# A Strassen-Winograd output projection that opens with two direct products, with its activation operands formed a stage earlier

## The chip, the cores and the metric

The kernel runs on one core of a Trainium2 chip. The metric is the device time of one execution in microseconds (us). The core's engines are TensorE (PE; its weight loads are listed as PEld), VectorE (DVE), ScalarE (ACT), GpSimd (POOL) and SyncE (SP). Each takes its instructions in its own order and waits for the others at semaphores. DMAs are issued here from SP (weights), from POOL (accumulating loads) and from ACT (a few row broadcasts).

## The reference

One layer over x of 512 tokens by 2048 channels, all in float32. Two mixers A and B work on the normalised input; their gated sum goes through w_out, whose result the change is about:

```python
y_a = o_a @ w_br_a[i]
...
u = jax.nn.silu(layernorm(u, ln_g[i], ln_b[i])) * jax.nn.silu(z_b)
y_b = u @ w_br_b[i]
gate_a, gate_b = jnp.split(jax.nn.sigmoid(gate_logits + b_gate[i]), N_BRANCHES, axis=-1)
mixed = (gate_a * y_a + gate_b * y_b) @ w_out[i]
x = x + rmsnorm(mixed, g_post[i])
e = p[i] @ w_ple_proj[i]
x = x + rmsnorm(jax.nn.sigmoid(x @ w_ple_gate[i]) * e, g_ple[i])
```

## The kernel before, in words

Every matrix product is done in three matmuls. An operand is split into a high part (hi: a cast on ScalarE) and a low part (lo: operand minus hi, a subtraction on VectorE), and hi by hi, hi by lo and lo by hi are added in PSUM. Weights come by DMA and are split just ahead of their matmuls.

The program runs the stages one after the other: normalisation and transposes, heads of branch A, the convolution of branch B, the gate and output tiles of branch A, then branch B, w_out, and the last gemm with its norms. In branch B the normalised input hT (in hpool, 32 buffers) gives sixteen gate tiles (gate_b), and the convolved uT gives sixteen output tiles (yb, from w_br_b); each is 48 matmuls. When a yb tile is done, VectorE multiplies it by its gate (L818) and adds it to the tile of mixed (L820). In the order of the code, two gate tiles run ahead, then one gate tile and one yb tile in turn.

w_out multiplies mixed (512 by 2048) by a 2048 by 2048 matrix in Strassen-Winograd form: two column halves (jp) of seven products each, P1, Q5, P6, P7, P3, P2, Q4, instead of eight. The halves of the tokens and of the channels make four blocks of activations, and four of weights for each jp (B11, B12, B22, B21). The activation operands are A11 for P1, S1 for Q5, S2 for P6, S3 for P7, S4 for P3 (sums of blocks), A12 for P2 and A22 for Q4 (both in CC). split_a forms A11 and S1 between the last yb tiles and the start of w_out; split_b (S3, S2, S4) is stepped along with the pieces of P1 and Q5, split_c (CC) with those of P6, P7 and P3.

A *piece* is one quarter q of the rows of one product's weights: 128 by 1024, 512 KB, with 12 matmuls (L1034, L1035, L1036). Its source is either a loaded block (L950, from SP), or a sum. The sum t = B11 + B12 (VectorE, L964) serves Q5; then an accumulating DMA from POOL (L956) adds B22 to it for P6, and later B21 for Q4. t3 = B12 + B22 (L973) serves P7. split_piece makes a piece's hi (L1010) and lo (L1011); next_piece_sw keeps three or four pieces split ahead. Where a source is a sum, next_piece_sw issues its loads and at once, behind them, the sum.

Loads go to ring buffers (raw, three; shared with the stages before) or to rw (four); t has four buffers, the split halves lie in ring (w, four), wx (two) and later raw. A buffer is loaded anew when its last reader is done, and SP takes its loads in order. When products end, their PSUM tiles are copied (snap, L1056) or added on VectorE (L1060, L1064), squared and summed on ScalarE (L1079), and multiplied by the row g_post (grow, loaded from ACT's queue; L1080). After the last products come the norm and the transposes of the result (L1107, L1113).

The order of each engine's instructions is set at compile time by a scheduler that starts from the order of the code and moves instructions by their dependencies; what is written in a generator and stepped is spread over the steps by hand.

Of the kernel before, what the change touches and what calls it, by code (L numbers as in the profile page):

```python
# [15 lines left out]
P = 128  # L16
# [65 lines left out]
def _body(ctx, tc, A, out):  # L82
# [756 lines left out]
    def split_a():  # L839
        for k2 in range(4):  # L840
            ah = hpool.tile([P, T], F32R, tag="h", name="ah")
            al = hpool.tile([P, T], F32R, tag="h", name="al")
            s1 = slots.tile([P, T], F32, tag="s", name="sf")
            for n in range(2):
                kk = 2 * k2 + n
                while not (kk in added and kk + 8 in added):
                    yield
                c = slice(n * 256, n * 256 + 256)
                nc.vector.tensor_tensor(s1[:, c], mixed[kk][:, HI], mixed[kk + 8][:, HI], ALU.subtract)
                nc.scalar.copy(ah[:, c], mixed[kk][:, LO])  # L850
                nc.vector.tensor_tensor(al[:, c], mixed[kk][:, LO], ah[:, c].bitcast(F32), ALU.subtract)
                yield
            Sf[k2] = s1
            AW["A11"][k2] = (ah, al)
            AW["S1"][k2] = sw_split(hpool, "h", s1)
            yield

    def split_b():
        for k2 in range(4):
            s1 = Sf.pop(k2)  # L860
            s3_ = s3.tile([P, T], F32, tag="s3", name="sf")
            for n in range(2):
                kk = 2 * k2 + n
                c = slice(n * 256, n * 256 + 256)
                nc.vector.tensor_tensor(s3_[:, c], mixed[kk][:, LO], mixed[kk][:, HI], ALU.subtract)
                nc.vector.tensor_tensor(s1[:, c], s1[:, c], mixed[kk][:, LO], ALU.subtract)
            AW["S3"][k2] = sw_split(hpool, "h", s3_)
            yield
            AW["S2"][k2] = sw_split(hpool, "h", s1)
            for n in range(2):  # L870
                kk = 2 * k2 + n
                c = slice(n * 256, n * 256 + 256)
                nc.vector.tensor_tensor(s1[:, c], mixed[kk + 8][:, LO], s1[:, c], ALU.add)
            AW["S4"][k2] = sw_split(slots, "s", s1)
            yield
# [20 lines left out]
    lnp_ctx = ExitStack()
# [42 lines left out]
    entries = deque()  # L939
    sources = deque()  # L940
# [3 lines left out]

    def load(jp, blk, q):
        if early[0]:
            raw = ring.tile([P, 1024], F32, tag="raw", name="raw", bufs=3)
        else:
            raw = s3.tile([P, 1024], F32, tag="rw", name="rw", bufs=4)
        nc.sync.dma_start(raw, WO[jp, blk, q])  # L950
# [7 lines left out]
    def e_a(jp, q):  # L958
        early[0] = jp == 0
        b11 = load(jp, B11, q)  # L960
        b12 = load(jp, B12, q)
        early[0] = False
        t = tb[q] = s3.tile([P, 1024], F32, tag="t", name="t", bufs=4)
        nc.vector.tensor_tensor(t, b11, b12, ALU.add)  # L964
# [23 lines left out]
    def e_t(jp, q):
        return [tb[q]]

    def e_c(jp, q):
        return e_p2(jp, q) + [tb[q]]

    def split_piece():
# [4 lines left out]
        for m in range(2):  # L999
            if n < 8:  # L1000
# [142 lines left out]
    drain(gen)  # L1143
    u2 = [add(unit(S3_, "u2"), ps["P6"][t], s1[t]) for t in range(2)]
# [5 lines left out]
    ps = run(("P2", "Q4"))  # L1150
# [186 lines left out]
```

## Time and profile before

| | |
|---|---|
| median of 3 runs | 2549.19 us (2548.08 to 2549.82) |
| profiled execution | 2548.13 us, span 2546.4 us |
| granted TensorE clock, mean | 0.998 |
| busy: PE / PEld / DVE / ACT / POOL | 98 / 80 / 65 / 42 / 6 % of the span |
| DMA moved | 279.45 MB, mean 110 GB/s |
| w_out begins | at 2188 us (last L818 at 2188.14, first matmul at 2188.98) |

Times in the profile are microseconds from the start of the span, unless marked ns. "Idle before, releaser" is the time for which an engine stood still just ahead of an instruction, and the instruction or DMA that let it go. Lines are those of the kernel before unless the change is spoken of.

### The profile page before, as it was taken

The page shows a single profiled execution, that of the slowest core. Times are in us where ns is not written, and L with a number is a line of the kernel's source. Part 1 is how long each engine was busy: PE and PEld are TensorE (multiplying, and loading weights), DVE is VectorE, ACT ScalarE, POOL GpSimd, SP SyncE. Part 2 cuts the span into 40 slices and gives each one's busy share as a digit, 9 for nine tenths or more (in the row PEclk, how much of TensorE's full clock was granted, in tenths as well). Part 3 has the DMA queues.
Part 4 walks back from the last instruction along what each step waited for, and adds up shares of the span by engine and source line. Part 5 has one row for each costly group of instructions (what it writes and reads, how often), then busy time and mean ns, then how long its engine had stood idle before and what let it go on. Part 6 is the DMA issues. An engine that isn't in the chain of part 4 may idle for free.

```text
span 2546.4 us, 32634 instructions
## 1 busy us (share of the span) xinstructions
PE 2503.4 (98%) x12202; PEld 2032.5 (80%) x12202; DVE 1650.9 (65%) x3092; ACT 1058.2 (42%) x2083; POOL 140.4 (6%) x151
## 2 busy tenths in 40 slices
PE   8999999999999999999999999999999999899998
PEld 7878787777878777888888888887888888687886
DVE  6766767666676765977786868947423333787744
ACT  6655455455545545322222222225422222454532
POOL 0100000000000000000000000002000000000000
PEclk9999999999999999999999999999999999999999
DMA  6322222222222222333333333342322223577642
GB/s 256 118 90 71 84 74 80 79 78 84 71 83 72 83 69 81 103 101 106 98 104 100 103 108 96 108 161 91 100 98 93 99 91 99 165 218 213 216 173 75
DMA packets 85406, 279.45 MB, mean 110 GB/s; under 512 B 9472, under 2 KB 9728, under 8 KB 85248
## 3 DMA queue, kind: packets, MB, share of 16 engines
q1 hardware_dynamic: 81792, 266.89, 31.3%
q0 software_dynamic: 2304, 8.39, 1.9%
q10 hardware_dynamic: 1152, 2.10, 0.3%
q8 instruction: 95, 1.56, 0.3%
q14 instruction: 63, 0.52, 0.1%
HBM read 262.66 MB, written 14.68 MB: 109 GB/s over the span
## 4 chain that ended last, share of the span: by engine, by line
PE 84%; DVE 9%; ACT 2%; issue 2%; DMA 2%; POOL 0%; SPq 0%; DVEq 0%; POOLq 0%; ACTq 0%
PE g L180 22%; PE g L178 22%; PE g L176 22%; DVE prod L589 2%; DVE w L124 2%; PE f L1191 2%; PE f L1192 2%; PE f L1190 2%; DVE VT L590 2%; PE psS L467 1%; PE f L1035 1%; PE f L1036 1%; PE f L1034 1%; DVE cv L404 1%; PE psB L462 1%
## 5 line engine op out<-in xcount | busy, mean ns | idle before, releaser
L180 PE MATMUL g<-hh,w 128*128 128x512 f32 x2320 | 919.4, 396 | 13.2 <-DVE w L124 13.2
L178 PE MATMUL g<-hl,w 128*128 128x512 f32 x2320 | 915.9, 395 | 0.0
L176 PE MATMUL g<-hh,w 128*128 128x512 f32 x2320 | 914.5, 394 | 0.0
L124 DVE TENSOR_TENSOR w<-raw,w 128x512 fp32r<-128x512 f32 x780 | 547.8, 705 | 491.8 <-ACT w L123 490.7
L123 ACT CAST w<-raw 128x512 fp32r<-128x512 f32 x780 | 479.1, 620 | 899.2 <-PE g L180 822.6
L180 PEld LDWEIGHTS g<-hh,w 128*128 128x128 f32 x2320 | 436.7, 188 | 107.0 <-DVE w L124 21.4
L178 PEld LDWEIGHTS g<-hl,w 128*128 128x128 f32 x2320 | 436.6, 188 | 87.3 <-issue 1.6
L176 PEld LDWEIGHTS g<-hh,w 128*128 128x128 f32 x2320 | 436.6, 188 | 83.7 <-issue 0.2
L671 DVE SCALAR_TENSOR_TENSOR uc<-sg,vec,uc 128x483 f32<-128x483 f32 (+15 forms) x480 | 351.3, 734 | 14.2 <-ACT uc L668 4.3
L404 DVE SCALAR_TENSOR_TENSOR cv<-g,vec,cv 128x511 f32<-128x511 f32 x144 | 107.0, 743 | 32.9 <-ACT cv L402 32.3
L180 PE MATMUL g<-uh,w 128*128 128x512 f32 x256 | 100.9, 394 | 0.0
L176 PE MATMUL g<-oh,w 128*128 128x512 f32 x256 | 100.9, 394 | 0.0
L178 PE MATMUL g<-ol,w 128*128 128x512 f32 x256 | 100.9, 394 | 0.0
L180 PE MATMUL g<-oh,w 128*128 128x512 f32 x256 | 100.9, 394 | 0.0
L176 PE MATMUL g<-uh,w 128*128 128x512 f32 x256 | 100.9, 394 | 0.0
L178 PE MATMUL g<-ul,w 128*128 128x512 f32 x256 | 100.9, 394 | 0.0
L589 DVE TENSOR_TENSOR prod<-UT,VT 128x2 f32<-128x2 f32 (+30 forms) x248 | 87.8, 354 | 7.2
L1034 PE MATMUL f<-wsp,oph 128*128 128x512 f32 x192 | 74.9, 394 | 3.2 <-ACT wsp L1010 3.2
L1035 PE MATMUL f<-wsp,oph 128*128 128x512 f32 x192 | 75.7, 394 | 1.5 <-DVE wsp L1011 1.5
L1191 PE MATMUL f<-w,xh 128*128 128x512 f32 x192 | 75.1, 391 | 0.1
L1036 PE MATMUL f<-wsp,opl 128*128 128x512 f32 x192 | 75.1, 391 | 0.0
L1192 PE MATMUL f<-w,xl 128*128 128x512 f32 x192 | 75.0, 390 | 0.0
(297 smaller groups left out, 2678.2 us busy)
## 6 DMA issues: line engine op xcount, KB each, us to landing
raw<-in_w_in SPq DMA_DIRECT2D x290, 512.0 KB, 3.3
raw<-in_w_ple_gate SPq DMA_DIRECT2D x40, 512.0 KB, 4.0
rw<-in_w_out SPq DMA_DIRECT2D x36, 512.0 KB, 5.0
raw<-in_w_br_a SPq DMA_DIRECT2D x32, 512.0 KB, 3.3
raw<-in_w_br_b SPq DMA_DIRECT2D x32, 512.0 KB, 3.2
t<-in_w_out POOLq DMA_DIRECT2D x16, 512.0 KB, 7.3
x<-in_x SPq DMA_DIRECT2D x8, 512.0 KB, 9.4
pe_dram<-e_sb SPq DMA_DIRECT2D x16, 256.0 KB, 5.6
```

The lines of the kernel that those rows point to most:

```text
L123: nc.scalar.copy(hi, rq)
L124: nc.vector.tensor_tensor(lo, rq, hi.bitcast(F32), ALU.subtract)
L176: mm(ps, wh, rh, start=(k == 0), stop=False)
L178: mm(ps, wh, rl, start=False, stop=False)
L180: mm(ps, wl, rh, start=False, stop=(k == NK - 1))
L404: nc.vector.scalar_tensor_tensor(y[:, s:], ps[:, 0:T - s], vv(w0 + 3 - s), y[:, s:], ALU.mult, ALU.add)
L589: nc.vector.tensor_tensor(pv_, um, vm, ALU.mult)
L671: nc.vector.scalar_tensor_tensor(y[:, s:], u[:, 0:T - s], vv(w0 + TAPS - 1 - s), y[:, s:], ALU.mult, ALU.add)
L1035: mm(ps, lh, wl[:, c], start=False, stop=False)
L1036: mm(ps, ll, wh[:, c], start=False, stop=kk == 7)
L1191: mm(ps[tt], lh, wl, start=False, stop=False)
L1192: mm(ps[tt], ll, wh, start=False, stop=k == NK - 1)
```

## The change

Three things are changed.

1. In branch B eight gate tiles run ahead instead of two (six of the first eight, and all later ones, in the pool s2 instead of slots), so the last eight yb tiles stand one after the other, and hT's buffers are free before them. In these tiles combine(k2) forms A11, CC, S1, S2 and S4 for k2 = 0, 1, 2, one step every 12 matmuls. combine(3) and the splits of S3 stand beside P1 and P2, two steps for each piece.
2. The first column half begins with P1 and P2 in turn, straight from loaded B11 and B21. Then Q5 runs alone, with B11 loaded a second time beside B12 for t; then P6, P7, P3 as before; then Q4. P2's result is finished early. The first half has 24 plain loads instead of 20; the accumulating ones are as before, 16 in all. The second half keeps its order.
3. An entry is now two steps: its loads, and a function that does its sum. The loads of an entry are issued two entries ahead of its sum (started). Only the first three loads use the ring's raw buffers, and the pieces up to the ninth alternate between ring and wx. The rows of x for the last norm (xr) go to slots.

```diff
-    def evac_gate(dst, i, col):
+    def evac_gate(dst, i, col, pool=None):
         def f(ps):
-            gt = slots.tile([P, T], F32, tag="s", name="gt")
+            gt = (pool or slots).tile([P, T], F32, tag="s2" if pool else "s", name="gt")
...
-    def split_a():
...
+    def combine(k2):
+        ah = hpool.tile([P, T], F32R, tag="h", name="ah")
+        al = hpool.tile([P, T], F32R, tag="h", name="al")
+        for kk, c in halves(k2):
+            while not (kk in added and kk + 8 in added):
+                yield
+            nc.scalar.copy(ah[:, c], mixed[kk][:, LO])
+            nc.vector.tensor_tensor(al[:, c], mixed[kk][:, LO], ah[:, c].bitcast(F32), ALU.subtract)
+            yield
+        AW["A11"][k2] = (ah, al)
+        for kk, c in halves(k2):
+            CC[kk] = sw_split(hpool, "h", mixed[kk + 8])
+            yield
+        s1 = slots.tile([P, T], F32, tag="s", name="sf")
+        for kk, c in halves(k2):
+            nc.vector.tensor_tensor(s1[:, c], mixed[kk][:, HI], mixed[kk + 8][:, HI], ALU.subtract)
+        AW["S1"][k2] = sw_split(hpool, "h", s1)
+        yield
+        s3_ = slots.tile([P, T], F32, tag="s", name="sf")
+        s4 = slots.tile([P, T], F32, tag="s", name="sf")
+        for kk, c in halves(k2):
+            nc.vector.tensor_tensor(s3_[:, c], mixed[kk][:, LO], mixed[kk][:, HI], ALU.subtract)
+            nc.vector.tensor_tensor(s1[:, c], s1[:, c], mixed[kk][:, LO], ALU.subtract)
+        yield
+        for kk, c in halves(k2):
+            nc.vector.tensor_tensor(s4[:, c], mixed[kk + 8][:, LO], s1[:, c], ALU.add)
+        AW["S2"][k2] = sw_split(slots, "s", s1)
+        yield
+        AW["S4"][k2] = sw_split(slots, "s", s4)
+        Sf[k2] = s3_
+        yield
+
+    def split_mixed():
+        for k2 in range(3):
+            yield from combine(k2)
+
+    def split_s3():
         for k2 in range(4):
-            ah = hpool.tile([P, T], F32R, tag="h", name="ah")
-            al = hpool.tile([P, T], F32R, tag="h", name="al")
...
-            AW["S1"][k2] = sw_split(hpool, "h", s1)
...
-    def split_b():
-        for k2 in range(4):
...
-    def split_c():
-        for kk in range(8):
-            CC[kk] = sw_split(*((slots, "s") if kk < 4 else (s3, "s3")), mixed[kk + 8])
+            AW["S3"][k2] = sw_split(s3, "s3", Sf.pop(k2))
             yield
 
...
-    gate_b_tile(order[0])
-    gate_b_tile(order[1])
+    AHEAD = 8
+
+    def gate_b_tile(i, pool):
+        gemm_cm(w_in_tile(GATE_TILE0 + 16 + i), hT, evac_gate(gate_b, i, 16 + i, pool))
+
+    gate_b_tile(order[0], None)
+    gate_b_tile(order[1], None)
     jobs.append(finish)
+    for n in range(2, AHEAD):
+        gate_b_tile(order[n], s2)
     for n, i in enumerate(order):
-        if n + 2 < NK:
-            gate_b_tile(order[n + 2])
-        elif n == NK - 2:
-            jobs.append(lambda: spawn(split_a(), 6, "mix"))
         gemm_cm(A["w_br_b"][i], uT, evac_yb(i))
+        if n + AHEAD < NK:
+            gate_b_tile(order[n + AHEAD], s2)
+        elif n + AHEAD == NK:
+            jobs.append(lambda: spawn(split_mixed(), 12, "mix"))
...
+    started = deque()
...
     def load(jp, blk, q):
-        if early[0]:
+        loads[0] += 1
+        if loads[0] <= 3:
             raw = ring.tile([P, 1024], F32, tag="raw", name="raw", bufs=3)
         else:
             raw = s3.tile([P, 1024], F32, tag="rw", name="rw", bufs=4)
         nc.sync.dma_start(raw, WO[jp, blk, q])
         return raw
...
+    def e_p1p2(jp, q):
+        two = [load(jp, B11, q), load(jp, B21, q)]
+        return lambda: two
+
+    def sum_t1(jp, q):
         b11 = load(jp, B11, q)
         b12 = load(jp, B12, q)
-        early[0] = False
-        t = tb[q] = s3.tile([P, 1024], F32, tag="t", name="t", bufs=4)
-        nc.vector.tensor_tensor(t, b11, b12, ALU.add)
-        return [b11, t]
+
+        def f():
+            t = tb[q] = s3.tile([P, 1024], F32, tag="t", name="t", bufs=4)
+            nc.vector.tensor_tensor(t, b11, b12, ALU.add)
+            return [b11, t]
+        return f
+
+    def e_q5(jp, q):
+        f = sum_t1(jp, q)
+        return lambda: f()[1:]
 
     def e_63(jp, q):
...
-            if n < 8:
+            if n < 9:
...
     def next_piece_sw():
         ahead = 3 if count[0] < 10 else 4
-        while len(pieces) < ahead and (sources or entries):
-            while len(sources) < 2 and entries:
-                sources.extend(entries.popleft()())
+        while len(pieces) < ahead and (sources or entries or started):
+            while len(sources) < 2 and (entries or started):
+                while entries and len(started) < 2:
+                    started.append(entries.popleft()())
+                sources.extend(started.popleft()())
             split_piece()
...
-                xr[tt, j] = unit(HP_, "xr")
+                xr[tt, j] = unit(SLOT, "xr")
...
-    for e, jp in ((e_a, 0), (e_b, 0), (e_c, 0), (e_a, 1), (e_63, 1), (e_p2, 1), (e_p7, 1), (e_t, 1)):
+    for e, jp in ((e_p1p2, 0), (e_q5, 0), (e_b, 0), (e_q4, 0), (sum_t1, 1), (e_63, 1), (e_p2, 1), (e_p7, 1), (e_t, 1)):
         stage(e, jp)
 
-    gen = split_b()
-    ps = run(("P1", "Q5"), stepper(gen))
+    def opening():
+        yield from combine(3)
+        yield from split_s3()
+
+    gen = opening()
+    ps = run(("P1", "P2"), stepper(gen, 2))
     drain(gen)
     s1 = [snap(S3_, x) for x in ps["P1"]]
-    s5 = [snap(S3_, x) for x in ps["Q5"]]
+    c11 = [add(unit(S3_, "c11"), ps["P2"][t], s1[t]) for t in range(2)]
     gp = [bcast_row(A["g_post"], j) for j in (0, 1)]
     fin = out_fin(0, gp)
-    gen = split_c()
-    ps = run(("P6", "P7", "P3"), stepper(gen))
-    drain(gen)
-    u2 = [add(unit(S3_, "u2"), ps["P6"][t], s1[t]) for t in range(2)]
+    for t in range(2):
+        fin(t, 0, c11[t])
+    ps = run(("Q5",))
+    s5 = [snap(S3_, x) for x in ps["Q5"]]
+    ps = run(("P6", "P7", "P3"))
+    u2 = [add(s1[t], ps["P6"][t], s1[t]) for t in range(2)]
     d = [minus(unit(S3_, "d"), s5[t], u2[t]) for t in range(2)]
     u3 = [add(u2[t], ps["P7"][t], u2[t]) for t in range(2)]
     for t in range(2):
         fin(t, 1, add(d[t], ps["P3"][t], d[t]))
         fin(2 + t, 1, minus(s5[t], s5[t], u3[t]))
-    ps = run(("P2", "Q4"))
-    for t in range(2):
-        fin(t, 0, add(s1[t], ps["P2"][t], s1[t]))
+    ps = run(("Q4",))
     for t in range(2):
         fin(2 + t, 0, add(u3[t], ps["Q4"][t], u3[t]))
 
```

The three places below are those that the prediction speaks of. A name with a number is one instance of a tile: raw and rw are loaded blocks, t a sum, wsp a half of a piece, sf, oph and opl an operand's sum, hi and lo, c11 the result of P2 with its snap.

SP where w_out's loads begin, before:

```order
L118 DMA raw<-in_w_br_b 128x1024 x6
L950 DMA raw<-in_w_out 128x1024 x3
L950 DMA rw<-in_w_out 128x1024 x2
L950 DMA raw<-in_w_out 128x1024 x2
L950 DMA rw<-in_w_out 128x1024
L950 DMA raw<-in_w_out 128x1024 x2
L950 DMA rw<-in_w_out 128x1024
L950 DMA raw<-in_w_out 128x1024
L950 DMA rw<-in_w_out 128x1024 x17
L1100 DMA xr<-in_x 128x512 x4
L950 DMA rw<-in_w_out 128x1024
```

and after:

```order
L118 DMA raw<-in_w_br_b 128x1024 x16
L960 DMA raw<-in_w_out 128x1024 x3
L960 DMA rw<-in_w_out 128x1024 x34
L1125 DMA xr<-in_x 128x512 x3
L960 DMA rw<-in_w_out 128x1024
L1125 DMA xr<-in_x 128x512 x2
L960 DMA rw<-in_w_out 128x1024
```

The loads that alternated between the two kinds of buffer now have three in raw, and all others pass through the four rw buffers; the loads of xr come later among them.

VectorE at the second and third sums t, before:

```order
L964 TENSOR_TENSOR t_17435<-raw_17431,raw_17433 128x1024
L836 TENSOR_TENSOR opl_17466<-sf_17459,oph_17464 128x512
L865 TENSOR_TENSOR sf_17518<-gt_9484 128x256
L836 TENSOR_TENSOR opl_17494<-sf_17245,oph_17492 128x512
L865 TENSOR_TENSOR sf_17575<-gt_9833 128x256
L1011 TENSOR_TENSOR wsp_17475<-t_17435,wsp_17474 128x1024
L873 TENSOR_TENSOR sf_17245<-gt_11033,sf_17245 128x256
L873 TENSOR_TENSOR sf_17245<-gt_11333,sf_17245 128x256
L964 TENSOR_TENSOR t_17472<-raw_17468,raw_17470 128x1024
L836 TENSOR_TENSOR opl_17500<-sf_17245,oph_17498 128x512
L1011 TENSOR_TENSOR wsp_17503<-raw_17468,wsp_17502 128x1024
```

Each t (L964) is followed by its lo (L1011), with the operands' sums and splits (L836, L865, L873) between them.

VectorE from the last P2 piece to the third piece of Q5, after:

```order
L1034 TENSOR_TENSOR wsp_17644<-rw_17526,wsp_17643 128x1024
L977 TENSOR_TENSOR t_17641<-rw_17583,rw_17585 128x1024
L1034 TENSOR_TENSOR wsp_17674<-t_17641,wsp_17673 128x1024
L977 TENSOR_TENSOR t_17671<-rw_17637,rw_17639 128x1024
L1085 TENSOR_TENSOR c11_17715<-f_17532,snap_17711 128x512
L1034 TENSOR_TENSOR wsp_17696<-t_17671,wsp_17695 128x1024
L977 TENSOR_TENSOR t_17693<-rw_17667,rw_17669 128x1024
L1085 TENSOR_TENSOR c11_17717<-f_17533,snap_17713 128x512
L977 TENSOR_TENSOR t_17734<-rw_17689,rw_17691 128x1024
L1105 TENSOR_TENSOR c11_17715<-c11_17715,grow_17719 128x512
L1105 TENSOR_TENSOR c11_17717<-c11_17717,grow_17719 128x512
L1034 TENSOR_TENSOR wsp_17737<-t_17693,wsp_17736 128x1024
```

The four sums (now L977) stand behind the eight direct pieces, and the lo (L1034) of the third Q5 piece, wsp_17737, stands behind the fourth sum and the two products of c11 with grow; the operands' rows are gone from here.

VectorE in the last three yb tiles, after:

```order
L820 TENSOR_TENSOR gt_12833<-gt_12833,gt_16556 128x512
L858 TENSOR_TENSOR sf_17570<-gt_10433,gt_12833 128x256
L864 TENSOR_TENSOR sf_17577<-gt_10433 128x256
L836 TENSOR_TENSOR opl_17548<-gt_12833,oph_17546 128x512
L124 TENSOR_TENSOR w_17364<-raw_17362,w_17364 128x512
L124 TENSOR_TENSOR w_17367<-raw_17362,w_17367 128x512
L124 TENSOR_TENSOR w_17409<-raw_17407,w_17409 128x512
L818 TENSOR_TENSOR gt_16690<-g_17316,gt_16690 128x512
L124 TENSOR_TENSOR w_17412<-raw_17407,w_17412 128x512
L820 TENSOR_TENSOR gt_10733<-gt_10733,gt_16690 128x512
```

The operands' sums and splits (L858, L864, L836) now stand between the weight splits (L124) and the evacuations (L818, L820) of branch B.

More of the change, by code (lines that the diff above doesn't have):

```diff
@@ L837, in sw_split @@
         return hi, lo
-    def split_a():
-        for k2 in range(4):
-            ah = hpool.tile([P, T], F32R, tag="h", name="ah")
-            al = hpool.tile([P, T], F32R, tag="h", name="al")
[L843 to L854, printed above, removed]
-            AW["S1"][k2] = sw_split(hpool, "h", s1)
-            yield
@@ L858, in split_b @@
-    def split_b():
-        for k2 in range(4):
[L860 to L875, printed above, removed]
@@ L877, in split_c, with halves @@
-    def split_c():
-        for kk in range(8):
-            CC[kk] = sw_split(*((slots, "s") if kk < 4 else (s3, "s3")), mixed[kk + 8])
+    def halves(k2):
+        for n in range(2):
+            yield 2 * k2 + n, slice(n * 256, n * 256 + 256)
+    def combine(k2):
[29 more added lines that the diff above has]
+        yield
@@ L880, in split_c @@
+    def split_mixed():
+        for k2 in range(3):
+            yield from combine(k2)
+    def split_s3():
+        for k2 in range(4):
+            AW["S3"][k2] = sw_split(s3, "s3", Sf.pop(k2))
             yield
     order = [k + 8 * n for k in range(8) for n in range(2)]
-    def gate_b_tile(i):
-        gemm_cm(w_in_tile(GATE_TILE0 + 16 + i), hT, evac_gate(gate_b, i, 16 + i))
-    gate_b_tile(order[0])
-    gate_b_tile(order[1])
+    AHEAD = 8
+    def gate_b_tile(i, pool):
+        gemm_cm(w_in_tile(GATE_TILE0 + 16 + i), hT, evac_gate(gate_b, i, 16 + i, pool))
@@ L943, in _body @@
     count = [0]
+    loads = [0]
     def load(jp, blk, q):
-        if early[0]:
+        loads[0] += 1
+        if loads[0] <= 3:
             raw = ring.tile([P, 1024], F32, tag="raw", name="raw", bufs=3)
@@ L951, in load, with sum_t3 @@
         return raw
-    early = [True]
     def acc(t, jp, blk, q):
         nc.gpsimd.dma_start(t, WO[jp, blk, q], accum_op=ALU.add)
-    def e_a(jp, q):
-        early[0] = jp == 0
+    def e_p1p2(jp, q):
+        two = [load(jp, B11, q), load(jp, B21, q)]
+        return lambda: two
+    def sum_t1(jp, q):
         b11 = load(jp, B11, q)
         b12 = load(jp, B12, q)
-        early[0] = False
-        t = tb[q] = s3.tile([P, 1024], F32, tag="t", name="t", bufs=4)
-        nc.vector.tensor_tensor(t, b11, b12, ALU.add)
-        return [b11, t]
+        def f():
[6 more added lines that the diff above has]
+        return lambda: f()[1:]
     def e_63(jp, q):
         acc(tb[q], jp, B22, q)
-        return [tb[q], load(jp, B22, q)]
-    def sum_t3(jp, q, b22):
-        b12 = load(jp, B12, q)
+        b22 = load(jp, B22, q)
+        return lambda: [tb[q], b22]
+    def sum_t3(b12, b22):
         nc.vector.tensor_tensor(b12, b12, b22, ALU.add)
@@ L978, in e_b, with e_q4 @@
         b22 = load(jp, B22, q)
-        return [tb[q], sum_t3(jp, q, b22), b22]
+        b12 = load(jp, B12, q)
+        return lambda: [tb[q], sum_t3(b12, b22), b22]
     def e_p7(jp, q):
-        return [sum_t3(jp, q, load(jp, B22, q))]
+        b22 = load(jp, B22, q)
+        b12 = load(jp, B12, q)
+        return lambda: [sum_t3(b12, b22)]
     def e_p2(jp, q):
         acc(tb[q], jp, B21, q)
-        return [load(jp, B21, q)]
+        b21 = load(jp, B21, q)
+        return lambda: [b21]
+    def e_q4(jp, q):
+        acc(tb[q], jp, B21, q)
+        return lambda: [tb[q]]
     def e_t(jp, q):
-        return [tb[q]]
-    def e_c(jp, q):
-        return e_p2(jp, q) + [tb[q]]
+        return lambda: [tb[q]]
     def split_piece():
```

## The prediction

> **What bounds the kernel now.** I read the profile's page first, then TensorE's waits, then windows around w_out, then the instructions at each stop.
>
> ```profile
> PE 2503.4 (98%) x12202; PEld 2032.5 (80%) x12202; DVE 1650.9 (65%) x3092; ACT 1058.2 (42%) x2083; POOL 140.4 (6%) x151
> ```
> TensorE is busy for 2503.4 of 2546.4 us, and the change removes no matmul. Only idle time, about 43 us, is to be had, and only what lies at the places that the change touches.
>
> ```profile
> PE f L1034 <- ACT wsp L1010: 3.9, 4, 2.0
> PE f L1035 <- DVE wsp L1011: 1.5, 2, 1.0
> PE f L1034 <- DVE gt L818: 0.9, 1, 0.9
> 2188.98 0.47 PE L1034 MATMUL f<-wsp,ah 128*128 128x512 f32 x1 [0.88 <-DVE gt L818]
> ...
> 2204.63 0.74 PE L1034 MATMUL f<-wsp,oph 128*128 128x512 f32 x2 [2.03 <-ACT wsp L1010]
> ...
> 2215.83 0.50 PE L1035 MATMUL f<-wsp,oph 128*128 128x512 f32 x1 [1.02 <-DVE wsp L1011]
> ...
> 2224.79 0.50 PE L1035 MATMUL f<-wsp,oph 128*128 128x512 f32 x1 [0.47 <-DVE wsp L1011]
> ```
> The first three rows are TensorE's waits between 2188 and 2260 us (total, times, longest); the others are four of its seven stops there, the first and the last among them. The stop at 2188.98 waits for the last evacuation of branch B (L818) and stays. The six later ones, 5.4 us of recorded idle, wait for the halves of a weight block.
>
> ```profile
> 2100.00:2188.00 88.00, 88.00 (x382) 71.09 (x380) 35.99 (x64) 24.34 (x44) 0.00 (x0) 1.00 0.28 90
> 2188.00:2226.00 38.00, 31.53 (x128) 23.37 (x128) 33.91 (x50) 21.21 (x30) 4.54 (x5) 1.00 0.80 212
> 2226.00:2260.00 34.00, 34.00 (x150) 27.94 (x150) 32.62 (x40) 20.25 (x30) 2.59 (x3) 1.00 0.69 197
> ```
> Columns: stretch, length, busy time and count of PE, PEld, DVE, ACT, POOL, then granted clock, DMA share, GB/s. From 2226 on, 150 matmuls take 34 us, 0.227 us each. At that rate the 128 of the middle row need 29.0 us, so 9.0 of 38 are lost: some 0.4 us more for each stop than the idle time says, since restarts are slow. With 1.2 us for the first stop (0.88 and its restart), **7.8 us can go**. The first row is the cover: in branch B, VectorE is busy 36 of 88 us, ScalarE 24, DMA 28%.
>
> Why TensorE stops:
>
> ```profile
> 2195.52 1.22 DVE L964 TENSOR_TENSOR t<-raw 128x1024 f32<-128x1024 f32 x1 [0.74 <-DMA raw<-in_w_out]
> ...
> 2202.22 1.23 DVE L964 TENSOR_TENSOR t<-raw 128x1024 f32<-128x1024 f32 x1 [1.79 <-DMA raw<-in_w_out]
> 2203.36 0.68 DVE L836 TENSOR_TENSOR opl<-sf,oph 128x512 fp32r<-128x512 f32 x1
> ...
> 2208.93 1.23 DVE L964 TENSOR_TENSOR t<-raw 128x1024 f32<-128x1024 f32 x1 [1.42 <-DMA raw<-in_w_out]
> 2196.82 0.93 SPq L950 DMA_DIRECT2D raw<-in_w_out  x2
> 2203.47 0.33 SPq L950 DMA_DIRECT2D raw<-in_w_out  x1
> 2193.88 1.06 POOL L956 DMA_DIRECT2D t<-in_w_out  x1 [435.65 <-DVE wsp L1011]
> ...
> 2200.07 0.87 POOL L956 DMA_DIRECT2D t<-in_w_out  x1 [5.12 <-DVE wsp L1011]
> ```
> The sum t = B11+B12 waits for its second load, and the hi and lo halves queue behind it. VectorE is nearly full, but half of its waits are for transfers: the bound here is load, sum, split in turn.
>
> **The change, part by part.**
>
> Operands moved into branch B (k2 = 0 to 2):
>
> ```profile
> L836 DVE TENSOR_TENSOR opl<-sf,oph 128x512 fp32r<-128x512 f32 x13 | 8.7, 682 | 0.0
> L865 DVE TENSOR_TENSOR sf<-gt 128x256 f32<-128x256 f32 x8 | 3.2, 416 | 0.0
> L834 ACT CAST oph<-sf 128x512 fp32r<-128x512 f32 x13 | 7.9, 619 | 5.1 <-DVE sf L865 2.3 <-DVE sf L873 1.9 <-DVE sf L849 1.0
> ```
> One combine(k2) issues on VectorE ten 128x256 at 0.416 and five 128x512 at 0.682, 7.6 us; on ScalarE five splits at 0.619 and two half-width copies, some 4 us. Three are 23 and 12 us, inside roughly 80 us of yb tiles with over half of VectorE free: I cost them at nothing. Weight pieces are split three ahead, and a step puts at most about 2 us in front of them. If that cover fails, L124 comes late as it does elsewhere:
>
> ```profile
> PE g L180 <- DVE w L124: 13.2, 10, 2.8
> ```
> Ten such stops cost 13.2 us, 1.3 each: bounds 0 and 3 us, taken 0. The gates only change place: the same matmuls, loads and evacuations, so 0.
>
> P1 and P2 as openers. Eight pieces come straight from loads, with no sum. A piece is 12 matmuls, 2.72 us, so piece n starts at about 2189.0+2.75n. Prices:
>
> ```profile
> L1011 DVE TENSOR_TENSOR wsp<-t,wsp 128x1024 fp32r<-128x1024 f32 x11 | 13.4, 1217 | 0.0
> L1010 ACT CAST wsp<-t 128x1024 fp32r<-128x1024 f32 x11 | 11.6, 1050 | 13.9 <-DVE t L964 8.8 <-PE f L1035 3.0 <-PE f L1036 1.9
> raw<-in_w_in SPq DMA_DIRECT2D x290, 512.0 KB, 3.3
> rw<-in_w_out SPq DMA_DIRECT2D x36, 512.0 KB, 5.0
> t<-in_w_out POOLq DMA_DIRECT2D x16, 512.0 KB, 7.3
> q1 hardware_dynamic: 2736, 9.96, 37.2%
> q0 software_dynamic: 1152, 4.19, 35.0%
> q10 hardware_dynamic: 288, 0.52, 2.3%
> DMA to landing us min/median/max: 6.0/7.3/7.7
> ```
> The queue rows are of 2188 to 2260 us and the last row of the grow loads. Over those 72 us, q1 is 19 loads, so 1.4 us of all engines each; q0 is 8 accumulating ones, 3.15 each; q10 two grow rows, 0.8 each. I let transfers pass in order of issue at these prices, each from 1.9 us after its issue (3.3 less 1.4). Tried on before: the accumulate of 2193.88 and the two loads of 2196.82 would be in at 2201.7 and the sum started at 2202.22; the accumulate of 2200.07 and the load of 2203.47 at 2207.7 (a third load of 2197.8 between), and the sum started at 2208.93. So transfers come 0.5 to 1.2 us later than reckoned; I add 1.0 at the end.
>
> Pieces 0 to 2 are loaded early. The next four loads now wait for the last L820, go out from 2190.7 and land from 2194.1 to 2198.8; pieces 3 to 7 are split 0.6 to 2 us before they are due, so even a lag of 1.0 costs 0.4 at most. So all six old stops go: **-7.8 us**.
>
> Q5 then becomes the narrow place. Its four pieces need two loads each, B11 a second time: four extra loads, 5.6 us of DMA. The rw buffers are four, so each pair is issued when an earlier block is done with:
> - The lo of piece 7 waits for piece 4's buffers (2202.75) and ends at 2205.1; only then goes the second Q5 pair's last load, landing at 2208.4. The second sum ends at 2209.6, and the last pair is issued.
> - The lo of the third Q5 piece (piece 10, due 2216.75) stands on VectorE behind the fourth sum and the two c11*grow products. The last pair lands near 2217.2 behind an accumulate. ScalarE issues the grow loads after piece 9's hi, 2210.7, landing at 2218 to 2219 by 7.3 us. Then two products (0.6 each) and the lo: 2221.3, **4.6 late**.
> - The lo of piece 11 stands behind L991, the first t3 sum, whose loads go out at 2214.1, beside the second accumulate: landing 2221.6 if ahead of it, 2224.8 if behind. With 1.2 for the sum and 1.2 for the lo: 2224.0 to 2227.2; due 2219.5 had nothing stopped, so the stage is 4.5 to 7.7 late.
>
> Being late counts once, so the larger applies; the middle of the second, 6.1, with the lag of 1.0 and 0.4 for a restart give **+7.5 us**, bounds 2.7 (all alone, rival A) and 10. Nearly all that was removed comes back.
>
> The rest: later pieces keep at least 2 us, since P6/P7/P3 needs 3.15+2.8 us of DMA per 8.2 us. The c11 work of P2 comes earlier; on the path it is the two products counted above. At the end of w_out there is one more stop:
>
> ```profile
> PE x1t L1113 <- DVE snap L1107: 2.4, 1, 2.4
> ```
> The sums in front of it hardly move, xr only changes buffers: 0, bounds -1 and +1.
>
> A rule against the change. At the program's start, before shows TensorE after a long stop:
>
> ```profile
> 6.24 0.80 PE L208 MATMUL e_ps<-w,ph 128*128 128x512 f32 x1 [6.24 <-ACT w L123]
> ...
> 8.41 0.63 PE L209 MATMUL e_ps<-w,ph 128*128 128x512 f32 x1
> 8.84 0.63 PE L210 MATMUL e_ps<-w,pl 128*128 128x512 f32 x1
> 11.40 0.51 PE L210 MATMUL e_ps<-w,pl 128*128 128x512 f32 x1
> 12.16 0.50 PE L208 MATMUL e_ps<-w,ph 128*128 128x512 f32 x1 [0.25 <-ACT ph L195]
> ```
> After 6.24 us idle, matmuls come every 0.43 us for 5.2 us, 12 of them, 2.4 us more than at 0.227; after 2.03 us (row at 2204.63) none does. A stop of 4.6 lies between: taken 0, upper end 2.4. The Trainium skill, "TensorE: Matmul & The Clock Gate", Part 1, says that after one idle window of about 3.4 us the clock falls to half until about 3.4 us are busy; by it the stop would cost an estimated 1.7 us more, and before's 2.03 us nothing.
>
> **Sum.** The profiled execution took 2548.13 us (its span is 2546.4, 1.7 lies around it): 2548.13 - 7.8 + 7.5 = 2547.8. The median of the runs shown, 2549.19, is 1.06 higher, so 2548.9.
>
> **Rivals.** A. *Q5 fits.* Loads land as alone (3.3), ahead of the accumulates, and grow in 6.0, at 2216.7; with two products and the lo piece 10 is ready at 2219.1, 2.3 late, 2.7 with the restart: 2549.2-7.8+2.7 = 2544.1. For it: lone loads do so. Against: the DMA share of 0.80 over 38 us in before, with fewer loads. B. *Slower: the transfers jam at Q5.* Loads for L991 land late:
>
> ```profile
> DMA to landing us min/median/max: 3.2/5.0/19.0
> ```
> That is rw over the whole program. At 19.0 from 2214.1, L991 starts at 2233.1, the lo ends at 2235.5, 16 us late: 2549.2-7.8+16.4 = 2557.8. It ends slower from a landing of about 15.5 us on (12.9 us lost). Against: the 19 stood where more loads were outstanding, in the second column half. C. *Cold restart*, as in the rows above: 2548.9+2.4 = 2551.3. By the Trainium skill's rule named above it would be near 2550.6. D. *The gain is taken in branch B*: combine's bursts delay L124 by up to 3 us: 2551.9; its steps come only every 12 matmuls, against.
>
> **How the numbers follow.** Forecast (Q5 loses 4 to 10 us) 0.52; A 0.2; B 0.08; C 0.12; D 0.08. A measurement of this kernel can tell about 0.2%, 5.1 us, from no change: faster is under 2544.1, slower over 2554.3. A stands on that line: 0.15 of its 0.2 (with the -1 at the end of w_out) go to faster; B with 0.03 from C and D, with 10 us lost at Q5 and their own price (2551.4+2.4 or 3), gives slower 0.11; the rest, 0.74, is same. The range runs from A with the -1 at the end of w_out (2543) to C with 10 us lost at Q5, its price halved (2552.6, so 2552.5).
>
> **What would show it.** Right: the six stops between 2197 and 2226 are gone, and one or two, 4 to 9 us together, stand at 2216 to 2226, at the third and fourth Q5 pieces, released by the lo half; VectorE idles there before the t sum (L977), L1105 or L991 for DMA; VectorE's share rises by some 20 us in branch B without a TensorE stop. Wrong: no stop over 2 us at Q5 (A), stops over 13 us (B), 0.43 us spacing behind the stop (C), more stops at L180 before 2188 (D).

## The result: 5.5 us slower, by one stop at Q5 and the half clock behind it

Over 20 runs each, the changed kernel took 2553.19 us (median), the kernel before 2547.66; ratio 1.0021, 95% interval 1.0014 to 1.0028. The profiled execution of the changed kernel has a span of 2552.2 us. The page's busy row and TensorE's waits (engine, line, releaser: us in total, times, longest):

```profile
PE 2503.8 (98%) x12202; PEld 2034.2 (80%) x12202; DVE 1652.1 (65%) x3092; ACT 1060.3 (42%) x2083; POOL 140.6 (6%) x151
PE g L180 <- DVE w L124: 13.1, 10, 2.8
PE f L1060 <- DVE wsp L1034: 11.8, 3, 9.9
...
PE x1t L1138 <- DVE c L1132: 1.4, 1, 1.4
```

Lines L1059 to L1061 are now the matmuls of w_out, L1033 and L1034 the halves, L1132 the norm's product. The six stops of before are gone; one of 9.9 us has come at Q5, and two small ones at the end of w_out (below). By stretch (columns as in the prediction):

```profile
2187.00:2215.00 28.00, 27.44 (x120) 22.43 (x120) 22.96 (x29) 15.27 (x23) 1.93 (x2) 1.00 0.78 241
2215.00:2233.00 18.00, 7.66 (x21) 5.51 (x20) 10.23 (x10) 4.82 (x6) 2.61 (x3) 0.62 0.92 256
2233.00:2260.00 27.00, 27.00 (x119) 22.15 (x118) 13.43 (x13) 11.54 (x12) 2.59 (x3) 1.00 0.88 220
```

P1 and P2 run without a stop (120 matmuls in 28 us). In the 18 us of the second row only 21 matmuls run, 4.8 us of work: 13.2 us are lost there, and the granted clock is 0.62 in the mean. TensorE's timeline shows both parts:

```profile
2215.76 0.73 PE L1059 MATMUL f<-wsp,oph 128*128 128x512 f32 x2 [0.44 <-ACT wsp L1033]
2226.39 0.79 PE L1060 MATMUL f<-wsp,oph 128*128 128x512 f32 x1 [9.90 <-DVE wsp L1034]
2226.98 0.63 PE L1061 MATMUL f<-wsp,opl 128*128 128x512 f32 x1
...
2231.68 0.57 PE L1061 MATMUL f<-wsp,opl 128*128 128x512 f32 x1
2232.08 0.39 PE L1059 MATMUL f<-wsp,oph 128*128 128x512 f32 x1
```

The stop is at the lo half of the third Q5 piece. From 2226.39 to 2232.08 thirteen matmuls take 5.7 us instead of 3.0. Behind the stop stands one transfer; the timelines of VectorE, SP, POOL and ACT's queue, the landing of the pair of loads that SP issued at 2209.20 and 0.4 us later, and the DMA queues from 2209 to 2223 us (packets, MB, share of the 16 engines; q1 has SP's loads, q0 the accumulating ones, q10 those of grow):

```profile
2212.19 1.23 DVE L977 TENSOR_TENSOR t<-rw 128x1024 f32<-128x1024 f32 x1 [0.67 <-DMA rw<-in_w_out]
...
2222.77 1.23 DVE L977 TENSOR_TENSOR t<-rw 128x1024 f32<-128x1024 f32 x1 [8.76 <-DMA rw<-in_w_out]
2223.91 1.29 DVE L1105 TENSOR_TENSOR c<-c,grow 128x512 f32<-128x512 f32 x2
2225.12 1.22 DVE L1034 TENSOR_TENSOR wsp<-t,wsp 128x1024 fp32r<-128x1024 f32 x1
2209.20 0.83 SPq L960 DMA_DIRECT2D rw<-in_w_out  x2
DMA to landing us min/median/max: 9.0/11.0/13.1
2208.07 1.06 POOL L964 DMA_DIRECT2D t<-in_w_out  x1 [451.16 <-DMA rw<-in_w_out]
2211.83 0.87 POOL L964 DMA_DIRECT2D t<-in_w_out  x1 [2.70 <-DVE wsp L1034]
2209.22 0.89 ACTq L930 DMA_DIRECT2D grow<-in_g_post  x2
q1 hardware_dynamic: 639, 2.35, 45.2%
q0 software_dynamic: 288, 1.05, 40.9%
q10 hardware_dynamic: 288, 0.52, 14.0%
```

The fourth sum waits 8.76 us for a load that landed 13.1 us after its issue. In these 14 us the DMA engines had no time free, and SP's loads got less than half of it. Two products with grow and the lo half follow, as the prediction had the order. w_out as a whole (first matmul to last) took 167.7 us before and 175.0 after.

### The profile page after: what moved, and what is told of

Its sections match the earlier page's. It is cut to its first block, busy times and chain, and to the rows that moved or that the text cites. A ratio compares the mean times of both kernels' runs of the same rounds, so it can differ in the third digit from the quotient of the medians.

```text
span 2552.2 us, 32646 instructions
## 1 busy us (share of the span) xinstructions
PE 2503.8 (98%) x12202; PEld 2034.2 (80%) x12202; DVE 1652.1 (65%) x3092; ACT 1060.3 (42%) x2083; POOL 140.6 (6%) x151
## 4 chain that ended last, share of the span: by engine, by line
PE 82%; DVE 10%; issue 3%; ACT 2%; DMA 2%; POOL 0%; SPq 0%; DVEq 0%; POOLq 0%; ACTq 0%
PE g L178 22%; PE g L180 22%; PE g L176 22%; DVE prod L589 3%; DVE w L124 2%; DVE VT L590 2%; PE f L1221 2%; PE f L1220 2%; PE f L1219 2%; PE psS L467 1%; PE f L1060 1%; PE f L1061 1%; PE f L1059 1%; DMA rw<-in_w_out 1%; DVE cv L404 1%
## 5 line engine op out<-in xcount | busy, mean ns | idle before, releaser
L180 PE MATMUL g<-hh,w 128*128 128x512 f32 x2320 | 919.5, 396 | 13.1 <-DVE w L124 13.1
L124 DVE TENSOR_TENSOR w<-raw,w 128x512 fp32r<-128x512 f32 x780 | 547.6, 705 | 476.5 <-ACT w L123 474.9
L180 PEld LDWEIGHTS g<-hh,w 128*128 128x128 f32 x2320 | 436.7, 188 | 106.5 <-DVE w L124 21.3
L180 PE MATMUL g<-uh,w 128*128 128x512 f32 x256 | 100.9, 394 | 0.0
L180 PE MATMUL g<-oh,w 128*128 128x512 f32 x256 | 100.9, 394 | 0.0
L1059 PE MATMUL f<-wsp,oph 128*128 128x512 f32 x192 | 75.9, 396 | 0.5 <-ACT wsp L1033 0.4
L1061 PE MATMUL f<-wsp,opl 128*128 128x512 f32 x192 | 76.3, 397 | 0.0
```

The lines of the kernel that those rows point to most:

```text
L124: nc.vector.tensor_tensor(lo, rq, hi.bitcast(F32), ALU.subtract)
L180: mm(ps, wl, rh, start=False, stop=(k == NK - 1))
L1061: mm(ps, ll, wh[:, c], start=False, stop=kk == 7)
```

## The experiments

Ratios are to the kernel before, run on the same chip in the same session.

### e1_no_acc and e12_no_acc2: what held the pair up

```diff
     def e_b(jp, q):
-        acc(tb[q], jp, B22, q)
+        if q > 1:          # e12_no_acc2: if q != 1
+            acc(tb[q], jp, B22, q)
```

> Leaves out the two accumulating loads (B22 onto the first two sums t) that are issued while the fourth pair of Q5's loads is under way, at 2208.07 and 2211.83 in the changed kernel; P6 then lacks B22 in two quarters. Theory S (transfers in flight share the 16 DMA engines whatever their order of issue): both took some 3 us of all engines, so the fourth pair lands about 4 to 6 us earlier than 13.1 us after its issue, at 7 to 9, and the 9.9 us stop shrinks to about 4 to 6; with it the half clock behind the stop goes or shortens. Rival F (transfers go in order of issue): only the accumulate issued before the pair stood in its way: 3 us earlier, stop about 7. Rival V (VectorE's order, not the transfers, sets the stop): no change beyond 1 us.

> Of the two accumulating loads left out in e1_no_acc, only the second is left out here: the one that the changed kernel issues 2.3 us after the fourth Q5 pair (P6 lacks B22 in one quarter). Theory S2 (an accumulating load on its own queue takes its share of the engines from loads issued before it): the pair still lands about 3 us earlier than 13.1 us, and the 9.9 us stop falls to 6 to 7.5. Rival F (what is issued later does not delay what is issued before): landing and stop as in the changed kernel, within 1 us.

Without both accumulating loads: ratio 0.9999 (0.9989 to 1.0008). Without the second alone: 1.0013 (1.0004 to 1.0023). Landing of the fourth pair and TensorE's stop, first of e1_no_acc:

```profile
DMA to landing us min/median/max: 4.8/5.7/6.6
2218.42 0.80 PE L1061 MATMUL f<-wsp,oph 128*128 128x512 f32 x1 [3.14 <-DVE wsp L1035]
```

and of e12_no_acc2:

```profile
DMA to landing us min/median/max: 7.8/8.7/9.6
2222.96 0.80 PE L1061 MATMUL f<-wsp,oph 128*128 128x512 f32 x1 [7.20 <-DVE wsp L1035]
```

The last load lands 13.1, 9.6 and 6.6 us after its issue with two, one and no accumulating load: 3.5 and 3.0 us for them here, near the price that the prediction read from the queue's share. (In e4_warm below, with the same transfers as the changed kernel, it is 12.5, which gives an idea of how far such a landing varies.) The second is issued after the pair and still delays it. So an accumulating load on its own queue takes engine time from loads already under way. The 3 us are no constant, though: e3_fin_late and e6_dve_add give other sums. And the half clock did not go with the 9.9 us: behind the stop of 3.14 us the granted clock is 0.50 from 2219 to 2223 too.

### e2_gate_next: do later loads of the same queue do so too?

```diff
+        if late is not None:
+            nc.vector.tensor_copy(raw[:, 0:1], late[:, 0:1].bitcast(F32))
         nc.sync.dma_start(raw, WO[jp, blk, q])
```

The copy reads the lo half of the third Q5 piece; this kernel also issues loads one entry ahead. With one entry ahead alone, the compiled order of instructions on every engine is the same as the changed kernel's: the look-ahead moves nothing here.

> The next two loads (B22, B12 of the first quarter of P6/P7/P3), issued 4.3 us after the fourth Q5 pair in the changed kernel, are held back until the lo half of the third Q5 piece is made, by a one-column copy into their buffers on VectorE; all else stays. Theory S: they shared the engines with the pair, 1.4 us each of all engines: the pair lands 2 to 3 us earlier (10 to 11 us after issue), and the stop at the third Q5 piece shrinks by as much, to about 7; a new stop may come at the first P7 piece, whose loads are now late. Rival F: the pair is ahead of them in any case: no change of its landing (13.1) or of the stop (9.9).

Ratio 1.0050 (1.0035 to 1.0065). Landing of the pair, then two of TensorE's stops:

```profile
DMA to landing us min/median/max: 7.7/9.9/12.0
2223.20 0.80 PE L1063 MATMUL f<-wsp,oph 128*128 128x512 f32 x1 [9.36 <-DVE wsp L1037]
2236.04 1.25 PE L1062 MATMUL f<-wsp,oph 128*128 128x512 f32 x3 [3.34 <-ACT wsp L1036]
```

The pair lands 1.1 us earlier, not 2 to 3, and the stop keeps 9.4 us; the held loads make the new stop at 2236. Loads that SP issues later hardly slow those that it issued before. Sharing was the right idea for transfers of other queues only.

### e3_fin_late: the order on VectorE, and grow's loads

```diff
-    for t in range(2):
-        fin(t, 0, c11[t])
     ps = run(("Q5",))
     s5 = [snap(S3_, x) for x in ps["Q5"]]
     ps = run(("P6", "P7", "P3"))
+    for t in range(2):
+        fin(t, 0, c11[t])
```

The loads of grow move with it.

> The finish of c11 (squares, the two products with grow, and the two loads of grow) is moved behind P6/P7/P3. In the compiled order the lo half of the third Q5 piece then stands ahead of the fourth sum, with no wait for its loads. Theory: the stop moves from the third to the fourth Q5 piece, due 2.75 us later, and loses the two products (1.2) and grow's 1.6 us of transfers: from 9.9 to about 4 to 5.5 us; total 5 to 8 us below the changed kernel with the shorter restart. If the transfers alone decide, and neither VectorE's order nor grow matters, the stop keeps 9 to 10 us.

Ratio 1.0007 (0.9997 to 1.0016), by the two ratios some 3.6 us below the changed kernel, where 5 to 8 were expected; their intervals together leave about 1 to 7. TensorE's timeline, and the landing of the fourth pair, issued at 2210.74:

```profile
2221.68 0.51 PE L1059 MATMUL f<-wsp,oph 128*128 128x512 f32 x1 [2.06 <-ACT wsp L1033]
2222.94 0.80 PE L1060 MATMUL f<-wsp,oph 128*128 128x512 f32 x1 [0.76 <-DVE wsp L1034]
2223.54 0.63 PE L1061 MATMUL f<-wsp,opl 128*128 128x512 f32 x1
...
2228.66 0.63 PE L1061 MATMUL f<-wsp,opl 128*128 128x512 f32 x1
2229.08 0.44 PE L1059 MATMUL f<-wsp,oph 128*128 128x512 f32 x1
DMA to landing us min/median/max: 6.8/7.5/8.1
```

The stop moved to the fourth piece and fell to 2.8 us, more than expected; the slow matmuls stayed (fourteen from 2222.94 to 2229.08, 6.1 us for 3.2). But this run changes two things, and the larger one is not the order. Both accumulating loads are still there (issued at 2209.84 and 2213.36), and yet the pair lands 8.1 us after its issue instead of 13.1, as the two rows of grow no longer move beside it: the prediction had priced these at 0.8 us each, and they went with 5.0. That accounts for 5.0 of the 7.1 us by which the stops fell. The other 2.1, an estimate by this difference, are left for VectorE's order, by which the third piece waits for the fourth piece's loads, and for the two products. No run here moves grow's loads alone, or the order alone.

### e6_dve_add and e11_dve_fin: repairs that leave nothing out

```diff
-        acc(tb[q], jp, B22, q)
         b22 = load(jp, B22, q)
         b12 = load(jp, B12, q)
-        return lambda: [tb[q], sum_t3(b12, b22), b22]
+        def f():
+            nc.vector.tensor_tensor(tb[q], tb[q], b22, ALU.add)
+            return [tb[q], sum_t3(b12, b22), b22]
+        return f
```

e11_dve_fin has this and the edit of e3_fin_late.

> The changed kernel with P6's sums of the first half, t + B22, made on VectorE from the B22 that is loaded anyway, in place of four accumulating loads; all that is computed stays. Theory: as where two of them were left out: the fourth Q5 pair lands 6 to 7 us after its issue instead of 13, the stop falls from 9.9 to 3 to 4 us, ratio to before 0.999 to 1.001. Rival: the sums on VectorE (four of 1.2 us, the first ahead of the fourth piece's lo half) make VectorE late instead: stop 5 to 7 us, ratio 1.001 to 1.003.

> The changed order of products (P1 and P2, then Q5 alone) with both repairs: c11 finished behind P6/P7/P3, and P6's sums on VectorE in place of accumulating loads. Theory: the first takes the fourth sum out of the third piece's way, the second halves the pair's landing; together they leave no stop above 2 us and no half clock at Q5: 4 to 7 us below before, ratio 0.9972 to 0.9985. Rival (Q5 alone needs more loads than four buffers can bring in time, whatever else): a stop of 3 us or more stays, ratio above 0.999.

e6_dve_add: ratio 0.9999 (0.9990 to 1.0008). e11_dve_fin: 0.9976 (0.9967 to 0.9985), 2540.13 against 2546.30 us. The landing of the fourth pair and TensorE's stop in e6_dve_add, then that landing and TensorE's stops at Q5 in e11_dve_fin:

```profile
DMA to landing us min/median/max: 7.0/7.7/8.5
2219.25 0.80 PE L1063 MATMUL f<-wsp,oph 128*128 128x512 f32 x1 [5.65 <-DVE wsp L1037]
```

```profile
DMA to landing us min/median/max: 5.2/5.7/6.1
2215.87 0.49 PE L1062 MATMUL f<-wsp,oph 128*128 128x512 f32 x1 [0.44 <-ACT wsp L1036]
2217.13 0.50 PE L1063 MATMUL f<-wsp,oph 128*128 128x512 f32 x1 [0.77 <-DVE wsp L1037]
2220.68 0.50 PE L1063 MATMUL f<-wsp,oph 128*128 128x512 f32 x1 [0.53 <-DVE wsp L1037]
```

e6_dve_add's time came as expected, its stop did not (5.7, not 3 to 4): the pair landed 8.5 us after its issue, not 6 to 7, though no accumulating load was under way. In e11_dve_fin, with neither these nor grow's rows beside it, it landed after 6.1. So the two accumulating loads cost the pair 6.5 us (e1_no_acc) or 4.6 (e6_dve_add) beside grow's rows, but 2.0 without them (8.1 in e3_fin_late, 6.1 here): what one transfer costs another depends on what else is in flight. What makes the difference between 6.6 and 8.5 stays open. With both edits no stop over 0.8 us is left at Q5: the order of products as such shows no cost.

### e4_warm: the half clock

```diff
+                    if q == 2:
+                        spare = bank()
+                        lh, _ = mix_opnd("S1", 3, 0)
+                        for _ in range(40):
+                            mm(spare, lh, prev[0][:, :T], start=True, stop=True)
```

> 40 extra matmuls (9.1 us at 0.227) into a spare PSUM bank are put ahead of the third Q5 piece, in the time of the stop. Theory C (the granted clock falls to half in the stop and 13 matmuls run at 0.43 us behind it): the clock stays at 1.00, the matmuls behind the stop come every 0.23 us, and the program is about 2.6 us faster than the changed kernel, the stop itself shrinking by the 9 us that the matmuls fill. Rival: the slow restart is the price of waiting on the halves, not of the clock: no gain, the spacing of 0.43 stays.

Ratio 1.0033 (1.0021 to 1.0044), which the interval does not tell from the changed kernel's. TensorE and VectorE:

```profile
2223.48 0.50 PE L1060 MATMUL f<-wsp,oph 128*128 128x512 f32 x1 [1.21 <-DVE wsp L1034]
2243.89 0.80 PE L1060 MATMUL f<-wsp,oph 128*128 128x512 f32 x1 [3.59 <-DVE wsp L1034]
2241.47 1.23 DVE L991 TENSOR_TENSOR rw<-rw 128x1024 f32<-128x1024 f32 x1 [9.57 <-DMA rw<-in_w_out]
```

Behind the filled stop the matmuls run at full pace, as expected of the clock. But no time was saved: a later t3 sum waits 9.57 us for its load, TensorE stops there for 3.59 us, and the slow matmuls follow that stop. What the clock gave was taken back by the next late load. So the clock's 2.7 us are seen in the spacing, but no run shows them as a saving.

### e5_p1q5, e9_before_buf, e10_early_oldbuf: what took the old stops away

e5_p1q5 opens with P1 and Q5 as before, and keeps the rest of the change:

```diff
-    for e, jp in ((e_p1p2, 0), (e_q5, 0), (e_b, 0), (e_q4, 0), (sum_t1, 1), ...
+    for e, jp in ((sum_t1, 0), (e_b, 0), (e_c, 0), (sum_t1, 1), ...
...
-    ps = run(("P1", "P2"), stepper(gen, 2))
+    ps = run(("P1", "Q5"), stepper(gen, 2))
```

e9_before_buf is the kernel before with the new rule for buffers; e10_early_oldbuf is e5_p1q5 with the old rule:

```diff
-        if early[0]:
+        loads[0] += 1
+        if loads[0] <= 3:
             raw = ring.tile([P, 1024], F32, tag="raw", name="raw", bufs=3)
...
-            if n < 8:
+            if n < 9:
```

> Undoes the new order of products (w_out opens with P1 and Q5 in turn again, t formed once, 20 plain loads in the first half) and keeps the rest: gates eight ahead, operands formed in branch B, loads two entries ahead. Theory: Q5 alone behind P1/P2, with its second loads of B11, is what costs; the early operands take the old stops away. Then no stop over 2 us between 2197 and 2230, and 5 to 8 us below before (ratio 0.997 to 0.998). Rival (the early operands bring little, since the old stops waited for loads behind three buffers): four to six stops of 0.5 to 2 us remain, ratio 0.999 to 1.000.

> The kernel before with the changed kernel's buffers alone: only w_out's first three loads go to raw, all others to the four rw buffers, pieces up to the ninth alternate as there; operands still formed at the start of w_out, products in the old order. Theory O (the operands' 21 sums and splits on VectorE made the old stops): they stay, 4 to 8 us lost between 2197 and 2226, ratio 0.999 to 1.000. Rival B (the old stops waited for the third raw buffer): most go, ratio 0.998 to 0.9985, like e5_p1q5.

> e5_p1q5 with the buffers of before: loads of the first P1 and Q5 entries alternate between raw and rw as there. Theory O: the stops stay away, ratio 0.9975 to 0.9985. Rival B: stops of 0.5 to 2 us at the second, third and fourth sums t come back, in all 4 to 8 us, ratio 0.9995 to 1.0005. Both may hold in part: then 2 to 4 us of stops.

| products in the old order | operands late | operands early |
|---|---|---|
| old buffers | 1 (before) | 0.9999 (0.9990 to 1.0008) |
| new buffers | 0.9985 (0.9977 to 0.9994) | 0.9980 (0.9971 to 0.9989) |

The "early" column has the look-ahead and the new place of xr too. The buffers' rule does the work (its two parts, the loads' and the pieces', were not tried apart); the early operands show no gain alone, and beside the new buffers none that the intervals tell. TensorE's waits at the halves in the whole program, of e9_before_buf and of e5_p1q5:

```profile
PE f L1034 <- DVE wsp L1010: 2.3, 5, 0.7
```

```profile
PE f L1065 <- DVE wsp L1039: 0.5, 2, 0.3
```

and in e10_early_oldbuf, a sum t, two stops of TensorE behind it, and a window with its clock:

```profile
2201.79 1.23 DVE L978 TENSOR_TENSOR t<-raw 128x1024 f32<-128x1024 f32 x1 [2.52 <-DMA raw<-in_w_out]
2204.20 0.74 PE L1065 MATMUL f<-wsp,oph 128*128 128x512 f32 x2 [1.04 <-ACT wsp L1039]
2205.67 0.73 PE L1065 MATMUL f<-wsp,ah 128*128 128x512 f32 x2 [0.73 <-ACT wsp L1039]
2208.00:2210.00 2.00, 2.00 (x7) 1.52 (x5) 1.15 (x2) 0.00 (x0) 0.00 (x0) 0.50 1.07 240
```

With the old rule the sums wait for loads into raw, and the old stops are back (3.8 us in five), though VectorE has fewer operands to form there: combine(3) and the splits of S3 are left, and it is busy 29.6 us of the 38 from 2187, for 33.9 before. In e9_before_buf it has them all, and yet waits for no load from the last L818 until 2221.

### e8_p1q5_dve and e7_merged: other orders

e8_p1q5_dve is e5_p1q5 with the sums of e6_dve_add. e7_merged opens with P1 and P2 and runs the other four products in turn, so that one B12 serves t and t3:

```diff
-    ps = run(("Q5",))
+    ps = run(("Q5", "P7", "P6", "P3"))
     s5 = [snap(S3_, x) for x in ps["Q5"]]
-    ps = run(("P6", "P7", "P3"))
```

> The old order of products with early operands, and P6's sums on VectorE instead of accumulating loads. If the accumulates hurt only where they compete with loads that are waited for, as at Q5 alone: within 0.1% of the same kernel with them. If their traffic also makes stops here: 1 to 4 us below it.

> P1 and P2 in turn, then Q5, P7, P6, P3 in turn: the B12 loaded for t serves t3 too, t + B22 is a sum on VectorE, and c11 is finished late. So the first half has 20 plain loads and four accumulating ones, and a quarter of four pieces (11 us of matmuls) needs three loads, some 4.2 us of all DMA engines. Theory (Q5's pairs of loads beside the accumulates are the cost): no stop over 2 us in the first half, clock 1.00 there, 6 to 9 us below before, ratio 0.9965 to 0.9975. Rival (any sum that stands right behind the direct pieces comes late, since the four buffers free too late): a stop of 3 to 6 us at the first Q5 or P7 piece, ratio 0.999 to 1.000.

e8_p1q5_dve: 0.9976 (0.9965 to 0.9987), not told from e5_p1q5. e7_merged: 0.9991 (0.9983 to 1.0000); its first 75 us of w_out have no stop, but it gains less than expected, since a stop stands where Q4 and the second half's first pieces meet. TensorE there, and VectorE ahead of it:

```profile
2263.69 0.50 PE L1080 MATMUL f<-wsp,oph 128*128 128x512 f32 x1 [2.58 <-DVE wsp L1054]
2252.27 1.29 DVE L1125 TENSOR_TENSOR c<-c,grow 128x512 f32<-128x512 f32 x2 [3.40 <-DMA grow<-in_g_post]
2262.42 1.22 DVE L1054 TENSOR_TENSOR wsp<-t,wsp 128x1024 fp32r<-128x1024 f32 x1
```

VectorE first stands still 3.40 us for grow's load, then works without a break on the products' ends, with one other lo half among them, until the lo half of 2262.42, which is late. Whether that wait alone makes the stop was not tried, and where the rest of the expected gain went was not followed further.

## Why the prediction was wrong

The forecast was 2548.9 us, 2543 to 2552.5, same; measured were 2553.19 and a clear, small loss. It started from 2549.19 for the kernel before, of three runs; the twenty runs beside the changed kernel gave 2547.66. So the forecast for the change itself was -0.3 us and the measured change is +5.5: it missed by 5.8, more than the totals differ.

- *The six old stops go: right in size, not in cause.* The first row of the stretches above has nothing but the first stop. But in the old order of products the table shows that the rule for buffers takes most of them away, and the operands' place next to nothing. The prediction had read from the rows of L964 that the sums wait for their second load, and had left the buffers, the cheapest part of the change, without a term of their own. (Its "half of its waits are for transfers" counts the 4.3 us that VectorE stood for branch B's last tile; behind that, all its 3.9 us of waits up to 2226 are for loads.)
- *Branch B costs nothing: right.* The stops at L180 are 13.1 us in ten, 13.2 before. VectorE's added work there is seen in the windows, before and after:

```profile
1900.00:2188.00 288.00, 288.00 (x1251) 233.86 (x1249) 97.70 (x154) 74.86 (x125) 0.00 (x0) 1.00 0.28 94
```

```profile
1900.00:2187.00 287.00, 286.69 (x1242) 232.18 (x1240) 112.59 (x184) 81.90 (x136) 0.00 (x0) 1.00 0.28 94
```

  Fifteen us more of VectorE for 23 reckoned. No gain of rival D's kind was taken.
- *Q5 becomes the narrow place: right in place and order; the term was mis-sized, 7.5 us forecast and 13.2 measured with the clock.* The third piece's lo stood behind the fourth sum and the products with grow. The step that failed is "The last pair lands near 2217.2 behind an accumulate": the load landed at 2222.7. The prediction let transfers pass in order of issue. So only one accumulate stood ahead of the pair, and the loads of grow, which it put at 2210.7, behind it. The runs show that transfers of other queues share the engines with the pair whatever their place: the second accumulate, issued 2.3 us after the pair, cost it 3.5 us (e12_no_acc2), and with grow's loads, issued in fact at 2209.22 together with the pair, went 5.0 us (e3_fin_late). These parts do not add up, and how much each costs with other transfers beside it stays open. VectorE's order, which cost the third piece what only the fourth needed, was foreseen; its part is the smaller one.
- *Cold restart (rival C, 0.12, priced 2.4 and taken as 0): it came, 2.7 us.* The rule cited there, from the Trainium skill's "TensorE: Matmul & The Clock Gate", Part 1, agrees with this stop in that the clock fell after 9.9 us idle. Its length does not: the spacing was 0.43 us for 5.7 us, not some 3.4, and cost 2.7 us, for the estimated 1.7. The step that failed is taking 0 between stops of 2.03 and 6.24 us when the range of the stop itself reached to 10.
- *The end of w_out: taken 0, bounds -1 and +1; measured +1.7.* The stop at x1t fell from 2.4 to 1.4 us, but two at the halves (0.57 and 1.36 us, with 0.4 each for the restart) came just ahead of it. No run shows which part of the change makes them.

By the runs' terms: 7.8 removed, 13.2 lost at Q5 with the restart and the clock, 1.9 more just before x1t with 0.4 for each of two restarts, and 1.0 less at x1t. That is +7.1 by these terms, +7.3 by the length of w_out. The stretch before w_out was 1.4 us shorter in this profile; in the kernels here the first matmul of w_out starts anywhere from 2184.8 to 2189.1 us, so that part need not be an effect of the change. The profiled executions as a whole differ by 6.5 us, the medians by 5.5.

## What to carry to other kernels

Before costing a transfer at its place in its queue, look for what other queues have in flight with it: here the pair landed 13.1 us after its issue beside two accumulating loads and two short rows, 8.1 without the rows, and 6.6 without the accumulating loads. Where a sum waits for a load, look on its engine at what stands behind it. And of several edits made together, try the smallest alone: a few lines on buffers gave 0.9985. The new order of products gave nothing until both faults at Q5 were mended, and its 0.9976 then is not told from 0.9985 by the intervals.

## What the runs showed of the hardware that was not expected

- The half clock does not need one long stop. In e3_fin_late it followed stops of 2.06 and 0.76 us with one matmul between them; in e10_early_oldbuf the granted clock was 0.50 from 2208 to 2210 after stops of 1.04 and 0.73 us with others of 0.76 and 0.53 us some 6 to 8 us before. A single stop of 2.03 us (before) or 2.58 us (e7_merged) brought none. Nor do the lengths of the stops alone decide it: at the end of w_out the same two stops, of about 1.05 and 1.4 us and 2.6 us apart, had a granted clock of 0.50 behind them in e1_no_acc (2337 to 2340) and in e8_p1q5_dve (2332 to 2335), and of 1.00 in e3_fin_late (2340 to 2343) and in e11_dve_fin (2334.3 to 2337.3). By the Trainium skill's rule named above ("TensorE: Matmul & The Clock Gate", Part 1) it takes one idle window of some 3.4 us; e3_fin_late and e10_early_oldbuf, with no single stop that long, do not agree with that, and what sums up the stops is not known from these runs.
- Loads that wait behind others of their own queue hardly slow them (e2_gate_next: 12.0 for 13.1 us), but transfers of other queues do, and those issued later as well (e12_no_acc2: 9.6 for 13.1). Two rows of grow, 0.52 MB in all and 14% of the engines' time from 2209 to 2223, went with 5.0 us of the pair's landing (e3_fin_late): more than their own time on the engines, 2.0 us, an estimate from that share.
